# FFN down projection: weight sums formed beside the products instead of during gate/up

## The chip, the core and the metric

One core of a Trainium2 chip runs the whole program. The metric is the device time of one execution in microseconds (us), lower is better; the number compared is the median of several runs. Engines: TensorE (PE, its weight loads PEld), VectorE (DVE), ScalarE (ACT), GpSimd (POOL), and SyncE (SP), which here only issues DMAs. SPq, ACTq and POOLq are the queues on which SP, ACT and POOL issue transfers.

## The reference, cut to what matters

```
x  = x + g1 * (merged @ w_out)
xn = modulate(rmsnorm(x, norm2), sh2, sc2)
h  = gelu(causal_conv3(xn @ w_gate) + b) * (xn @ w_up)      # 1024 tokens x 2816
x  = x + g2 * (h @ w_down)                                  # w_down 2816 x 1024
out = rmsnorm(x, final_norm)
```

Everything is float32. `g2` is the last sixth of `silu(c) @ w_ada + b_ada`, a row of 1024 numbers. The layers before this point are not touched by the change.

## The kernel before, in words

Every float32 operand of a matmul is split in two: a rounded high part `h` (ACT, line 117) and the rest `l = x - h` (DVE or POOL, line 118). A product then takes three matmuls of 128x512: high by high, high by low, low by high. The large products are done on 2x2 blocks with seven block products instead of eight; for that, sums and differences of blocks are formed first.

**Gate/up** (the loop over `k` in `range(KH)`, KH = 11, lines 1281 to 1308). Each `k` computes two column groups of the gate and two of the up projection. For `k` = 0 a plain form is used, for `k` = 1 to 10 `unit_ws` (line 178 on) runs twice, 7 steps of 12 matmuls each (line 192), so 168 matmuls for each `k`. DVE forms block sums (line 149), splits (line 118), brings finished PSUM banks out (lines 164 to 173: `gp` is the gate result, `up` the up result), and does the convolution (1253) and the product with the gate (1261). POOL shares sums and splits. PE may write a bank again only when DVE or ACT has brought its content out.

Two generators run beside this, one step of each for every step of the units (`feed`, queues `side` and `rest`):

- `gate_row` (lines 1222 to 1246): the row `g2`. 16 loads of 128x512 of `w_ada` (`adaw`), each multiplied into an accumulator on DVE (`adaa`, lines 1232 and 1234), and four small matmuls (line 1242) that sum over the partitions, each followed by a DVE addition (1243) and a store.
- `down_weights` (lines 1206 to 1220), 44 times, for the FFN's down stage: two loads of `w_down` into a tile `dw` (two buffers), two DVE operations (1215, 1216), two POOL operations (1217, 1218), and a store of the four sums to the DRAM scratch `wd_scr` on POOL's queue (1219).

**Down** (lines 1312 to 1418). `w_down` is cut into blocks A11, A12, A21, A22, the hidden activations into B11 to B22. Seven products are run in the order A11·B11, A12·B21, S2·tb, S1·ta, S3·tc, S4·B22, A22·td, with S1 = A21 + A22, S2 = S1 - A11, S4 = A12 - S2, S3 = A11 - A21 read back from `wd_scr`. Each product has 11 rows `k`; a row loads a token block and a weight block (`raw`, four buffers, lines 1330 and 1331), splits both (`wh`, `wl`, eight buffers of each, so four rows), and runs 12 matmuls: three for each of four token tiles `tp` (line 1338), into four PSUM banks. The first product's banks are `x`; A12·B21 uses `y`, which shares its four banks with `z` of S1 and S4. After a product, its banks are copied (ACT) or added (DVE) into `part` tiles; `settle` (1348, 1349) multiplies by `g2` and adds to the residual rows `res`, and `finish_rows` does the final norm. The residual rows, `g2b` and `fnb` are loaded with ten DMAs of 512 KB on ACT's queue after the first product (lines 1374 to 1379).

A scheduler of the framework decides the order of the instructions on each engine from the program's order and its own time estimates; each engine then runs its list strictly in that order.

Of the kernel before, what the change touches and what calls it, by code (L numbers as in the profile page):

```python
# [20 lines left out]
P = 128  # L21
# [48 lines left out]
def trunk(ctx: ExitStack, tc: tile.TileContext, I: dict, out: bass.AP, dbg=None):  # L70
# [33 lines left out]
    wd_scr = [dram.tile([P, 4, HALF], F32, name=f"wd{k}_scr") for k in range(KH)]  # L104
# [1101 lines left out]
    def down_weights(pl, k, c):  # L1206

        w = pl.tile([P, 4, P], F32, tag="dw", bufs=2, name="dw")
        for h in range(2):
            r0 = (k + KH * h) * P  # L1210
            nc.sync.dma_start(w[:, 2 * h:2 * h + 2],
                              I["f_wdown"][r0:r0 + P].rearrange("p (h c) -> p h c", h=2)[:, :, P * c:P * c + P])
        yield
        a11, a21, a12, a22 = [w[:, j] for j in range(4)]
        dve.tensor_tensor(a21, a21, a22, op=OP.add)
        dve.tensor_tensor(a11, a21, a11, op=OP.subtract)
        pool.tensor_tensor(a22, a22, a11, op=OP.subtract)
        pool.tensor_tensor(a12, a12, a11, op=OP.subtract)
        nc.gpsimd.dma_start(wd_scr[k][:, :, P * c:P * c + P], w)
        yield  # L1220

    def gate_row(pl):

        for h in range(2):
            acc = pl.tile([P, HALF], F32, tag="adaa", bufs=1, name="adaa")
            c = 5 * D + HALF * h
            for k in range(KD):
                w = pl.tile([P, HALF], F32, tag="dw", bufs=2, name="adaw")
                nc.sync.dma_start(w, I["w_ada"][k * P:(k + 1) * P, c:c + HALF])
                yield  # L1230
                if k == 0:
                    dve.tensor_scalar(acc, w, cond[:, k:k + 1], None, op0=OP.mult)
                else:
                    dve.scalar_tensor_tensor(acc, w, cond[:, k:k + 1], acc, op0=OP.mult, op1=OP.add)
                yield
            yield
            row = pl.tile([1, 256], F32, tag="grow", bufs=1, name="grow")
            for q in range(2):
                sl = slice(256 * q, 256 * q + 256)
                nc.sync.dma_start(row, I["b_ada"][c:c + HALF][sl].rearrange("(o n) -> o n", o=1))  # L1240
                pt = gb3()
                pe.matmul(pt[0:1, :256], ones[:, 0:1], acc[:, sl], start=True, stop=True)
                dve.tensor_tensor(row, row, pt[0:1, :256], op=OP.add)
                nc.sync.dma_start(g_rows[5][:, HALF * h + 256 * q:HALF * h + 256 * q + 256], row)
                row = pl.tile([1, 256], F32, tag="grow", bufs=1, name="grow") if q == 0 else None
            yield
# [30 lines left out]
    with (tc.tile_pool(name="ffg", bufs=1) as ffg, tc.tile_pool(name="ffy", bufs=1) as ffy,  # L1277
          tc.tile_pool(name="ffu", bufs=1) as ffu, tc.tile_pool(name="ff", bufs=1) as ff):
        rest.append(gate_row(ff))
        rest.extend(down_weights(ff, k, c) for k in range(KH) for c in range(4))  # L1280
# [25 lines left out]
        while side or rest:  # L1306
# [7 lines left out]
    STEPS = (("x", "B11", "A11"), ("y", "B21", "A12"), ("x", "tb", "S2"), ("z", "ta", "S1"), ("x", "tc", "S3"),  # L1314
             ("z", "B22", "S4"), ("x", "td", "A22"))
# [6 lines left out]
    def weight_rows(n, k):  # L1322
        if n[0] == "S":
            return wd_scr[k][:, ("S2", "S1", "S4", "S3").index(n)]
# [3 lines left out]
    def down_load(tn, wn, k):  # L1328
        raw = ring.tile([P, 2, HALF], F32, tag="raw", bufs=4, name="raw")
        nc.sync.dma_start(raw[:, 0], token_rows(tn, k))  # L1330
        nc.sync.dma_start(raw[:, 1], weight_rows(wn, k))
        return raw

# [27 lines left out]

    banks = {}
    for si, (bk, tn, wn) in enumerate(STEPS[:6]):
# [8 lines left out]
        if si == 0:  # L1372
            g2b = dn.tile([P, D], F32, name="g2b")
# [4 lines left out]
            for t in range(NT):  # L1378
                nc.scalar.dma_start(res[t], x2_scr[t])
# [61 lines left out]
```

## Time and profile before

| what | value |
|---|---|
| median of 3 runs | 2039.89 us (2035.96 to 2040.68) |
| the profiled execution's own time | 2032.08 us |
| its span | 2030.2 us |
| mean granted TensorE clock | 0.97 of full |
| PE busy over the span | 1904.2 us (94%), 9503 matmuls |
| DVE busy | 1321.1 us (65%) |
| ACT busy, POOL busy | 893.1 us (44%), 945.3 us (47%) |
| DMA moved | 346.01 MB, 170 GB/s on average |

The profile is of one execution. Busy shares are means over stages with different limits. Gate/up with `unit_ws` runs from about 1360 to 1814 us after the span's start, the down stage from 1800 to the end. A wait in brackets in a timeline row is the idle time of that engine just before the instruction and what ended it. The granted clock is either 0.5 (1.2 GHz) or 1.0 (2.4 GHz) at any moment; a stretch's number is the mean.

### The profile page before, as it was taken

To read this page: it belongs to the slowest core of one execution; us is meant where nothing else is said; L and a number is where in the kernel's file an instruction comes from. 1 tells how busy PE (TensorE), PEld (TensorE's weight loads), DVE (VectorE), ACT (ScalarE), POOL (GpSimd) and SP (SyncE) were. 2 spreads that over 40 slices of the span, in tenths; PEclk is the share of its full clock that TensorE was granted. 3 is DMA by queue.
4 is the path that set the end of the run, shared out by engine and by line. 5 is a ranking of instruction groups with operands and counts; after the bars stand their busy time and mean duration, and the time that the engine had idled before them with its cause. 6 is when DMAs were issued, how large, how long until landed. Compare 5 with 4: busy or idle time off the path is not lost.

```text
span 2030.2 us, 27898 instructions
## 1 busy us (share of the span) xinstructions
PE 1904.2 (94%) x9503; PEld 1544.7 (76%) x9503; DVE 1321.1 (65%) x2215; ACT 893.1 (44%) x1638; POOL 945.3 (47%) x1265
## 2 busy tenths in 40 slices
PE   6899998999898999999999989999988899999997
PEld 5668997766676778787787769977776678887886
DVE  6776666476636673555457675679877668665567
ACT  5345556554542334544444332444333333444444
POOL 6453444354354342345556673465666666400002
PEclk9899999999999999999999999998999899999999
DMA  9233333356968554888757255314655554358654
GB/s 325 71 119 130 128 120 121 120 177 200 287 191 232 187 174 151 218 173 212 175 145 190 85 187 207 126 31 151 189 183 176 181 173 139 104 180 287 207 187 176
DMA packets 294286, 346.01 MB, mean 170 GB/s; under 512 B 19343, under 2 KB 221187, under 8 KB 294144
## 3 DMA queue, kind: packets, MB, share of 16 engines
q1 hardware_dynamic: 249616, 219.74, 36.4%
q10 hardware_dynamic: 33744, 87.18, 12.1%
q0 software_dynamic: 10784, 37.31, 6.9%
q8 instruction: 75, 1.23, 0.2%
q14 instruction: 67, 0.55, 0.1%
HBM read 244.41 MB, written 99.75 MB: 170 GB/s over the span
## 4 chain that ended last, share of the span: by engine, by line
PE 62%; DVE 12%; DMA 10%; issue 7%; POOL 5%; ACT 2%; SPq 1%; ACTq 0%; DVEq 0%; POOLq 0%
PE g L192 24%; PE gp L889 8%; PE g L1338 7%; PE go L1146 5%; PE g L267 4%; PE sl L951 3%; PE g L216 3%; DMA dw<-in_f_wdown_dram 3%; PE tp L995 2%; DVE wl L118 2%; DMA raw<-in_w_in_dram 1%; POOL wl L118 1%; DMA wd_scr<-dw 1%; PE o L1024 1%; PE o L1027 1%
## 5 line engine op out<-in xcount | busy, mean ns | idle before, releaser
L192 PE MATMUL g<-xs,wh 128*128 128x512 f32 x2520 | 821.6, 408 | 56.1 <-DVE up L169 18.0
L192 PEld LDWEIGHTS g<-xs,wh 128*128 128x128 f32 x2520 | 485.2, 194 | 189.1 <-DVE up L169 19.7
L192 PE MATMUL g<-xs,wl 128*128 128x512 f32 x1260 | 506.1, 404 | 0.0
L117 ACT ACTIVATE wh<-raw 128x512 fp32r<-128x512 f32 (+2 forms) x385 | 225.2, 609 | 345.2 <-PE g L192 77.2
L118 POOL TENSOR_TENSOR wl<-st,wh 128x512 fp32r<-128x512 f32 x153 | 240.2, 1573 | 242.7 <-ACT wh L117 234.9
L118 DVE TENSOR_TENSOR wl<-raw,wh 128x512 fp32r<-128x512 f32 (+2 forms) x284 | 226.3, 814 | 148.3 <-ACT wh L117 147.5
L192 PEld LDWEIGHTS g<-xs,wl 128*128 128x128 f32 x1260 | 244.0, 194 | 61.5 <-issue 4.2
L117 ACT ACTIVATE wh<-st 128x512 fp32r<-128x512 f32 x204 | 126.5, 629 | 266.7 <-PE g L192 167.0
L118 POOL TENSOR_TENSOR wl<-raw,wh 128x512 fp32r<-128x512 f32 (+2 forms) x101 | 137.4, 1363 | 165.2 <-ACT wh L117 154.5
L149 POOL TENSOR_TENSOR st<-raw 128x512 f32<-128x512 f32 x102 | 154.4, 1518 | 92.3 <-DVE wl L118 64.9
L889 PE MATMUL gp<-oT,wh 128*128 128x512 f32 x512 | 169.7, 412 | 0.9 <-DVE ot L173 0.9
L267 PE MATMUL g<-wh,xs 128*128 128x256 f32 x672 | 126.0, 288 | 0.0
L959 ACT ACTIVATE pm<-pm,stat 128x128 f32<-128x128 f32 (+1 forms) x192 | 89.3, 468 | 51.0 <-DVE stat L956 46.1
L1356 POOL TENSOR_TENSOR ms<-ms 128x1 f32<-128x1 f32 x8 | 4.8, 603 | 224.5 <-ACT junk L1355 224.4
L267 PEld LDWEIGHTS g<-wh,xs 128*128 128x128 f32 x672 | 104.6, 189 | 4.1 <-issue 4.1
L889 PEld LDWEIGHTS gp<-oT,wh 128*128 128x128 f32 x512 | 89.4, 191 | 21.9 <-issue 7.7
L1338 PE MATMUL g<-wl,wh 128*128 128x512 f32 x264 | 103.7, 393 | 0.0
L1338 PE MATMUL g<-wh,wl 128*128 128x512 f32 x264 | 103.6, 392 | 0.0
L889 PE MATMUL gp<-oT,wl 128*128 128x512 f32 x256 | 102.0, 398 | 0.0
L1338 PE MATMUL g<-wh 128*128 128x512 f32 x264 | 96.5, 390 | 2.1 <-ACT wh L117 2.1
L267 PE MATMUL g<-wl,xs 128*128 128x256 f32 x336 | 95.1, 283 | 0.0
L956 DVE CUSTOM_DVE_ANT_0 pm<-sl,bt 128x128 f32<-128x128 f32 (+1 forms) x192 | 64.0, 378 | 45.2 <-PE sl L951 45.0
(297 smaller groups left out, 3510.9 us busy)
## 6 DMA issues: line engine op xcount, KB each, us to landing
raw<-in_w_in_dram SPq DMA_DIRECT2D x66, 512.0 KB, 5.2
adaw<-in_w_ada_dram SPq DMA_DIRECT2D x48, 256.0 KB, 5.4
g_scr<-ot ACTq DMA_DIRECT2D x24, 512.0 KB, 3.6
raw<-in_w_ada_dram SPq DMA_DIRECT2D x24, 512.0 KB, 4.0
qk<-q_scr POOLq DMA_DIRECT2D x12, 1024.0 KB, 6.8
qk<-k_scr POOLq DMA_DIRECT2D x24, 512.0 KB, 10.2
raw<-g_scr SPq DMA_DIRECT2D x24, 512.0 KB, 3.4
raw<-in_f_wgate_dram SPq DMA_DIRECT2D x22, 512.0 KB, 5.1
```

The lines of the kernel that those rows point to most:

```text
L117: act.activation(h, src, AF.Copy)
L118: l_eng.tensor_tensor(l, src, h.bitcast(F32), op=OP.subtract)
L149: engs[int(name[1]) - 1].tensor_tensor(s_, src.get(x_) if isinstance(x_, str) else x_, src.get(y_) if isinstance(y_, str) else y_, op=op)
L192: pe.matmul(banks[bk], a[:, k, :], b, start=(fresh and j == 0), stop=(j == 11), skip_group_check=True)
L216: pe.matmul(banks[i, h], a[:, k, :], b, start=(fresh and j == 0), stop=(not fresh and j == 11), skip_group_check=True)
L267: pe.matmul(banks[t2][bk][:, 256 * i:256 * i + 256], a[:, sl], b[:, k % 2, :], start=(fresh and i == 0 and j == 0), stop=(j == 11), skip_g ...
L889: pe.matmul(pt, a_[:, k % g, :], b_, start=(j == 0), stop=(j == 3 * n - 1))
L951: pe.matmul(sb[:, of:of + n], lq, kt[:, ks], start=(of == 0 and kt is kh), stop=(kt is kl), skip_group_check=True)
L956: dve.tensor_tensor_reduce(out=pm[:, of:of + n], in0=sb[:, of:of + n], in1=bt[:, cfg, 256 - n:], scale=1.0, scalar=3e38, op0=OP.add, op1=O ...
L959: act.activation(pm[:, of:of + n], pm[:, of:of + n], AF.Exp, scale=-1.0, bias=stt[:, cfg, 0, idx:idx + 1], accum_out=stt[:, cfg, 1, idx:id ...
L1146: pe.matmul(pt[:, :256], a_[:, sl], b_[:, k % 2, :], start=(j == 0), stop=(j == 3 * KD - 1))
L1338: pe.matmul(bank, a_[:, sl], b_, start=(start and j == 0), stop=(j == 2), skip_group_check=True)
```

## The change

`down_weights` and `wd_scr` are gone: nothing of the down weights is formed in gate/up. In the down stage each row of a product with an S weight now forms its sum on DVE just ahead of its split: S1 into one of 11 tiles `held` (A21 + A22, the latter loaded into `held`), S2 and S4 in place from it, S3 in a `st` tile (three buffers) into which A21 is loaded. So that each sum follows from the one before, the products are in the order S1, S2, S4, S3. With that order `y` is followed directly by `z`, in the same banks, and `x` of S3 by `x` of A22. `gate_row` loads one tile ahead, uses a tile four steps after its load, and has three empty steps after each use. The loads of `g2b`, `fnb` and `res` are asked for one row after the end of the first product, and `settle` (with `finish_rows`) runs as a generator, one token tile for each row of the following product. The tiles `last` come from a pool that opens when `held` is closed.

```diff
-    wd_scr = [dram.tile([P, 4, HALF], F32, name=f"wd{k}_scr") for k in range(KH)]
...
-    def down_weights(pl, k, c):
...
+        def fetch(i):
+            if i < 2 * KD:
+                h, k = divmod(i, KD)
+                raws[i] = pl.tile([P, HALF], F32, tag="adaw", bufs=2, name="adaw")
+                nc.sync.dma_start(raws[i], I["w_ada"][k * P:(k + 1) * P, 5 * D + HALF * h:5 * D + HALF * h + HALF])
+        fetch(0)
+        for i in range(2 * KD):
+            h, k = divmod(i, KD)
+            fetch(i + 1)
+            for _ in range(4):
                 yield
+            w = raws.pop(i)
...
-        rest.extend(down_weights(ff, k, c) for k in range(KH) for c in range(4))
...
-    STEPS = (("x", "B11", "A11"), ("y", "B21", "A12"), ("x", "tb", "S2"), ("z", "ta", "S1"), ("x", "tc", "S3"),
-             ("z", "B22", "S4"), ("x", "td", "A22"))
+    STEPS = (("x", "B11", "A11"), ("y", "B21", "A12"), ("z", "ta", "S1"), ("x", "tb", "S2"), ("z", "B22", "S4"),
+             ("x", "tc", "S3"), ("x", "td", "A22"))
...
+    held = [sums.tile([P, HALF], F32, tag="held", bufs=KH, name="held") for _ in range(KH)]
+
+    def weight_sum(wn, k, a):
+        if wn[0] == "A":
+            return a
+        if wn == "S3":
+            s_ = ring_tmp([HALF])
+            nc.sync.dma_start(s_, block_rows("A21", k))
+            dve.tensor_tensor(s_, a, s_, op=OP.subtract)
+            return s_
+        s_ = held[k]
+        if wn == "S1":
+            nc.sync.dma_start(s_, block_rows("A22", k))
+            dve.tensor_tensor(s_, a, s_, op=OP.add)
+        elif wn == "S2":
+            dve.tensor_tensor(s_, s_, a, op=OP.subtract)
+        else:
+            dve.tensor_tensor(s_, a, s_, op=OP.subtract)
+        return s_
...
+    def residual():
+        nc.scalar.dma_start(g2b, bcast_rows(g_rows[5], P, D))
...
+    def settle_all(c, t0, sl, finish=False):
+        for tp in range(4):
+            settle(c[tp], t0 + tp, sl)
+            if finish:
+                finish_rows(t0 + tp)
+            yield
...
-            ts_, ws = ring_split(raw[:, 0], [HALF], dve), ring_split(raw[:, 1], [HALF], dve)
+            ts_ = ring_split(raw[:, 0], [HALF], dve)
+            ws = ring_split(weight_sum(wn, k, raw[:, 1]), [HALF], dve)
             for tp in range(4):
                 down_mm(banks[bk][tp], ts_, ws, tp, fresh and k == 0)
+            feed(side)
```

Three places in the built order. The first is DVE in gate/up at a place where PE waits for the `up` bank of line 169, before:

```order
L149 TENSOR_TENSOR st_14492<-st_14465,raw_14242 128x512
L1215 TENSOR_TENSOR dw_14512<-dw_14512 128x128
L1216 TENSOR_TENSOR dw_14512<-dw_14512 128x128
L1215 TENSOR_TENSOR dw_14559<-dw_14559 128x128
L1216 TENSOR_TENSOR dw_14559<-dw_14559 128x128
L169 TENSOR_TENSOR up_13883<-g3_14117,up_13883 128x512
L164 TENSOR_TENSOR gp_14232<-g3_14273,gp_14232 128x512
L171 TENSOR_TENSOR up_13883<-up_13883,g3_14191 128x512
```

and the same place of a `k` in the change (line numbers are one lower there):

```order
L148 TENSOR_TENSOR st_14346<-st_14322,raw_14127 128x512
L168 TENSOR_TENSOR up_13818<-g3_14020,up_13818 128x512
L163 TENSOR_TENSOR gp_14117<-g3_14155,gp_14117 128x512
L170 TENSOR_TENSOR up_13818<-up_13818,g3_14082 128x512
L117 TENSOR_TENSOR wl_14300<-raw_14127,wh_14299 128x512
```

The four `dw` operations between the block sum and the bank are gone. The second place is the second half of the gate row on DVE, in the change (1224 and 1226 are the lines 1232 and 1234 of before, 1239 is 1243, 1248 is 1253):

```order
L1239 TENSOR_TENSOR grow_14344<-grow_14344,g3_14387 1x256
L1224 TENSOR_SCALAR adaa_14506<-adaw_14115,cond_369 128x512
L1248 SCALAR_TENSOR_TENSOR y_14278<-gp_14118,cols1_682,y_14278 128x1024
L1248 SCALAR_TENSOR_TENSOR y_14277<-gp_14117,cols1_682,y_14277 128x1024
L1226 SCALAR_TENSOR_TENSOR adaa_14506<-adaw_14409,cond_369,adaa_14506 128x512
L148 TENSOR_TENSOR st_14655<-st_14632,raw_14440 128x512
...
L1226 SCALAR_TENSOR_TENSOR adaa_14506<-adaw_14570,cond_369,adaa_14506 128x512
L1226 SCALAR_TENSOR_TENSOR adaa_14506<-adaw_14714,cond_369,adaa_14506 128x512
L168 TENSOR_TENSOR up_14122<-g3_14328,up_14122 128x512
L170 TENSOR_TENSOR up_14122<-up_14122,g3_14395 128x512
L1226 SCALAR_TENSOR_TENSOR adaa_14506<-adaw_14874,cond_369,adaa_14506 128x512
```

All eight uses of that half stand within 19 rows of DVE (a `k` has about 30), some three `k` later than before; the eight of the first half stand in the same rows of DVE's list as before. In the program's text they are spread over nine `k`, in the built order they are not. The four small matmuls stand 451 to 1050 PE rows later than before, away from the last `adaa` operation that they read. The third place is the start of the down stage: ACT in the change (1383 to 1386 are the loads, `raw_16461` is row 7 of the first product, `raw_16484` row 8),

```order
L116 ACTIVATE wh_16445<-raw_16438 128x512
L1383 DMA g2b_16286<-g2_scr_1057 128x1024
L1384 DMA fnb_16287<-in_final_norm_dram 128x1024
L1386 DMA res_16288<-x20_scr_159 128x1024
L116 ACTIVATE wh_16464<-raw_16461 128x512
L1386 DMA res_16289<-x21_scr_160 128x1024
L116 ACTIVATE wh_16468<-raw_16461 128x512
L1257 DMA ff10_scr_177<-up_15957 128x1024
L1386 DMA res_16290<-x22_scr_161 128x1024
```

where before all ten loads stand in one piece behind the split of row 10; and SP in the change (`raw_16621` is row 2 of the second product, `raw_16644` row 3):

```order
L1322 DMA raw_16621<-ff13_scr_180 128x512
L1323 DMA raw_16621<-in_f_wdown_dram 128x512
L1341 DMA held_16275<-in_f_wdown_dram 128x512
L1341 DMA held_16276<-in_f_wdown_dram 128x512
...
L1341 DMA held_16285<-in_f_wdown_dram 128x512
L1322 DMA raw_16644<-ff14_scr_181 128x512
L1323 DMA raw_16644<-in_f_wdown_dram 128x512
```

The ten loads start four rows earlier and are mixed with splits and stores, and the eleven `held` loads stand in one piece ahead of row 3 of the second product. PE's list is the same up to single places, but for the first rows of S1·ta: there it goes bank by bank, ten matmuls for the first bank before the first one for the second.

## Rows read from the trace of the kernel before

**Rows 1.** Busy time by stretch, all engines; then PEclk, DMA share, GB/s.

```profile
core 0: us, PE busy (x) PEld busy (x) DVE busy (x) ACT busy (x) POOL busy (x), PEclk, DMA share, GB/s
...
1380.00:1440.00 60.00, 56.28 (x235) 44.19 (x235) 56.66 (x65) 22.67 (x34) 30.19 (x26) 0.97 0.59 190
1440.00:1700.00 260.00, 231.29 (x938) 182.82 (x938) 188.67 (x241) 86.38 (x134) 183.24 (x207) 0.93 0.55 172
1700.00:1800.00 100.00, 100.00 (x437) 81.69 (x436) 66.14 (x76) 41.75 (x63) 42.72 (x30) 1.00 0.37 126
1820.00:1860.00 40.00, 37.93 (x161) 30.87 (x160) 18.48 (x30) 17.46 (x31) 0.00 (x0) 0.96 0.94 343
1860.00:2000.00 140.00, 140.00 (x619) 115.97 (x618) 89.31 (x142) 69.62 (x122) 0.87 (x1) 1.00 0.62 198
```

**Rows 2.** The same view for line 192 alone (the gate/up matmuls).

```profile
1380.00:1440.00 60.00, 55.03 (x231) 43.94 (x231) 0.97 0.59 190
1440.00:1700.00 260.00, 230.21 (x934) 182.65 (x934) 0.93 0.55 172
1700.00:1800.00 100.00, 100.00 (x437) 81.65 (x435) 1.00 0.37 126
```

**Rows 3.** Waits by engine, 1440 to 1700 us: total, times, longest.

```profile
PE g L192 <- DVE up L169: 18.0, 4, 6.4
...
PE g L1242 <- DVE grow L1243: 2.5, 1, 2.5
...
DVE dw L1215 <- DMA dw<-in_f_wdown_dram: 65.3, 29, 5.8
```

**Rows 4.** Timeline of DVE and PE, 1548 to 1559 us.

```profile
1550.92 1.32 DVE L1216 TENSOR_TENSOR dw<-dw 128x128 f32<-128x128 f32 x1
1556.83 0.29 DVE L1215 TENSOR_TENSOR dw<-dw 128x128 f32<-128x128 f32 x1 [4.59 <-DMA dw<-in_f_wdown_dram]
1557.37 0.68 DVE L169 TENSOR_TENSOR up<-g,up 128x512 f32<-128x512 f32 x1
...
1558.11 1.22 PE L192 MATMUL g<-xs,wh 128*128 128x512 f32 x2 [6.38 <-DVE up L169]
```

**Rows 5.** Busy time in the stretch of half clock behind that wait.

```profile
1555.40:1562.20 6.80, 4.09 (x10) 3.23 (x11) 5.33 (x7) 0.00 (x0) 3.01 (x5) 0.50 0.37 116
```

**Rows 6.** Groups of instructions, 1395 to 1705 us, and 1300 to 1425 us (last row).

```profile
L1242 PE MATMUL g<-adaa,ones 128*1 128x256 f32 x8 | 2.6, 432 | 4.7 <-DVE grow L1243 2.5 <-DVE adaa L1234 2.2
...
L118 DVE TENSOR_TENSOR wl<-raw,wh 128x512 fp32r<-128x512 f32 x27 | 30.9, 1144 | 0.0
...
L149 DVE TENSOR_TENSOR st<-st,raw 128x512 f32<-128x512 f32 x4 | 6.0, 1508 | 0.0
```

**Rows 7.** Groups of instructions, 1700 us to the end.

```profile
L118 DVE TENSOR_TENSOR wl<-raw,wh 128x512 fp32r<-128x512 f32 x141 | 92.3, 689 | 76.4 <-ACT wh L117 76.3
...
L117 ACT ACTIVATE wh<-raw 128x512 fp32r<-128x512 f32 x145 | 85.4, 627 | 113.4 <-PE g L1338 71.7 <-PE g L192 20.2 <-DMA res<-x_scr 10.6
...
L1349 DVE TENSOR_TENSOR res<-res,c 128x512 f32<-128x512 f32 x12 | 8.3, 690 | 0.0
```

**Rows 8.** Timeline of ACT at the residual loads, then a DVE row behind them.

```profile
1816.52 1.32 ACT L117 ACTIVATE wh<-raw 128x512 fp32r<-128x512 f32 x2 [2.08 <-PE g L1338]
...
1829.06 7.41 ACTq L1379 DMA_DIRECT2D res<-x_scr  x8
1836.57 3.24 ACT L117 ACTIVATE wh<-raw 128x512 fp32r<-128x512 f32 x6 [10.59 <-DMA res<-x_scr]
...
1848.75 4.81 DVE L118 TENSOR_TENSOR wl<-raw,wh 128x512 fp32r<-128x512 f32 x7 [1.29 <-ACT wh L117]
```

**Rows 9.** Line 1338 by stretch: the gap, the half clock, an undisturbed product.

```profile
1835.30:1837.80 2.50, 0.43 (x3) 0.03 (x1) 1.00 1.03 418
1838.70:1842.10 3.40, 3.40 (x10) 2.65 (x9) 0.50 1.02 407
1869.20:1899.20 30.00, 30.00 (x134) 24.82 (x134) 1.00 0.64 194
```

**Rows 10.** DMA issues, 1820 to 1860 us, then 1860 to 2000 us (last row): median us to landing.

```profile
res<-x_scr ACTq DMA_DIRECT2D x8, 512.0 KB, 9.1
...
raw<-in_f_wdown_dram SPq DMA_DIRECT2D x11, 256.0 KB, 4.8
```

More of the change, by code (lines that the diff above doesn't have):

```diff
@@ L1222, in gate_row @@
-    def gate_row(pl):
[L1224 to L1229, printed above, removed]
-                yield
[L1231 to L1234, printed above, removed]
+    def gate_row(pl):
+        raws = {}
+        def fetch(i):
[8 more added lines that the diff above has]
+            for _ in range(4):
+                yield
+            w = raws.pop(i)
+            if k == 0:
+                acc = pl.tile([P, HALF], F32, tag="adaa", bufs=1, name="adaa")
+                dve.tensor_scalar(acc, w, cond[:, k:k + 1], None, op0=OP.mult)
+            else:
+                dve.scalar_tensor_tensor(acc, w, cond[:, k:k + 1], acc, op0=OP.mult, op1=OP.add)
+            for _ in range(3):
@@ L1235, in gate_row @@
                 yield
-            yield
-            row = pl.tile([1, 256], F32, tag="grow", bufs=1, name="grow")
+            if k < KD - 1:
+                continue
             for q in range(2):
-                sl = slice(256 * q, 256 * q + 256)
-                nc.sync.dma_start(row, I["b_ada"][c:c + HALF][sl].rearrange("(o n) -> o n", o=1))
+                c = HALF * h + 256 * q
+                row = pl.tile([1, 256], F32, tag="grow", bufs=1, name="grow")
+                nc.sync.dma_start(row, I["b_ada"][5 * D + c:5 * D + c + 256].rearrange("(o n) -> o n", o=1))
+                yield
+                yield
@@ L1241, in gate_row @@
                 pt = gb3()
-                pe.matmul(pt[0:1, :256], ones[:, 0:1], acc[:, sl], start=True, stop=True)
+                pe.matmul(pt[0:1, :256], ones[:, 0:1], acc[:, 256 * q:256 * q + 256], start=True, stop=True)
                 dve.tensor_tensor(row, row, pt[0:1, :256], op=OP.add)
-                nc.sync.dma_start(g_rows[5][:, HALF * h + 256 * q:HALF * h + 256 * q + 256], row)
-                row = pl.tile([1, 256], F32, tag="grow", bufs=1, name="grow") if q == 0 else None
-            yield
+                nc.sync.dma_start(g_rows[5][:, c:c + 256], row)
@@ L1248, in conv @@
+                yield
     def conv(k, gp, ys):
@@ L1360, in finish_rows @@
             nc.sync.dma_start(out[0, t * P:(t + 1) * P, dsl], res[t][:, dsl])
+    g2b = dn.tile([P, D], F32, name="g2b")
+    fnb = dn.tile([P, D], F32, name="fnb")
+    res = [dn.tile([P, D], F32, tag="res", bufs=NT, name="res") for _ in range(NT)]
+    cs = {}
+    def residual():
+        nc.scalar.dma_start(g2b, bcast_rows(g_rows[5], P, D))
+        nc.scalar.dma_start(fnb, bcast_rows(I["final_norm"], P, D))
+        for t in range(NT):
+            nc.scalar.dma_start(res[t], x2_scr[t])
+        yield
+    def settle_all(c, t0, sl, finish=False):
[3 more added lines that the diff above has]
+                finish_rows(t0 + tp)
+            yield
     banks = {}
@@ L1406, in trunk @@
         for i in range(2):
-            h, l = [dn.tile([P, HALF], F32R, tag="last", bufs=4 * KH, name="last") for _ in range(2)]
+            h, l = [lp.tile([P, HALF], F32R, tag="last", bufs=4 * KH, name="last") for _ in range(2)]
             split_to(h, l, raw[:, i], dve)
```

64 lines of the change are left out of this document (20 added, 44 removed).

## The prediction

> **What bounds the kernel now.** I first read the busy time by stretch. PE is the engine to follow, since it works nearly without a gap where nothing disturbs it: in 1700 to 1800 us it is busy for the whole of 100 us at clock 1.00 and runs 437 gate/up matmuls of line 192 [rows 1, 2], so one takes 100 / 437 = 0.229 us. Held against that rate the other stretches show what they lose. In 1440 to 1700 there are 934 such matmuls, worth 934 x 0.229 = 213.7 us, so **46.3 us are lost**; in 1380 to 1440 there are 231, worth 52.9, so 7.1 are lost [rows 2]. POOL and DMA are busier there, DVE at 189 of 260 us is not full, and the clock is 0.93 and 0.97 [rows 1].
>
> Next the waits say who causes it. In 1440 to 1700, PE waits four times, 18.0 us in all, for DVE's line 169, which empties the up bank. DVE itself stands 65.3 us in 29 waits at line 1215, for the `dw` loads [rows 3]. The timeline joins the two: DVE waits 4.59 us for a `dw` load at 1556.83, line 169 stands right behind it on the same engine, and PE has been idle 6.38 us when it gets its bank [rows 4]. DVE takes its list in order, so a load asked for too late stops a bank that had nothing to do with it. The loss does not end there: in the 6.8 us that follow PE runs at clock 0.50, 1.2 GHz: busy 4.09 us, it does 10 matmuls where the undisturbed rate gives 30 [rows 5]. So the 46.3 us are the waits, the half clock behind them, and PE held at DVE's pace while it catches up.
>
> Last, the down stage. An undisturbed product there (132 matmuls) is worth 132 x 30 / 134 = 29.6 us, a row of 12 about 2.7 [rows 9], with DVE busy 89 of 140 us and POOL with a single instruction [rows 1]. Its one visible loss is near the second product: a gap of 2.5 us with three matmuls, then 3.4 us at clock 0.50 [rows 9], beside ten residual loads of 512 KB that take 9.1 us to land [rows 10] and that ACT stood 10.59 us for [rows 8]. PE is idle 2.07 us of 1820 to 1860 [rows 1], and 3.4 us at half clock lose 1.7: 3.8 us.
>
> **The change, part by part.**
>
> *The `dw` steps go.* 44 times two loads, two DVE and two POOL operations and a store. The engines' own time costs nothing: in 1700 to 1800 DVE does its block sums and evacuations without `dw` and PE loses nothing [rows 1]. What goes is the wait. Of the 46.3 us I take away what the gate row causes there and not `dw`: its small matmuls, 8 records of 432 ns [rows 6], half of them in this stretch, 1.7; its wait of 2.5 [rows 3]; and half of a half-clock stretch like the one of 3.4 us in rows 9, 1.7. That leaves 46.3 - 5.9 = 40.4. In the built order the up bank now follows the block sum directly, and behind neither stands an operation that waits for a load just asked for. **-40.4.**
>
> *The gate row.* It loses 5.9 in the one stretch and 7.1 in the other, 13.0 in all. The 3.5 us of the matmuls stay. Of the other 9.5 the earlier loads and the distance of the four matmuls from the last `adaa` should take all, but in the built order the second half stands bunched on DVE, each multiplication within a few rows of the next load, so a `dw`-like wait or two is left there. Bounds 0 and -9.5, between which no row decides; the middle, **-4.7**.
>
> *The start of the down stage.* The ten loads now start near 1818 (ACT splits of that row stand at 1816.52 [rows 8]). Before PE can start row 3 of the second product, near 1845, the queues must bring ten residual loads (5.2 MB), the store of the last activations (0.5) and of four token sums (1.05), eleven `held` loads of 256 KB (2.9), which stand on SP's queue ahead of that row's own loads, and five raw rows (2.6): 12.3 MB in 27 us. At the mean of 343 GB/s of 1820 to 1860 [rows 1] that takes 36 us, at the 407 to 418 of the worst moments [rows 9] about 30: PE is 3 to 9 us late. I take 5, the nearer to the high rate since the queue stands full, plus 1.7 for half clock behind it, against the 3.8 lost there now: **+2.9**. Bounds: -3.8 if nothing is late, and 9 + 3.4 - 3.8 = +8.6 at the mean rate with two stretches of half clock.
>
> The Trainium skill, "DMA: Bandwidth & Descriptors", section Specifications, gives a limit of about 358 GB/s for HBM for each core, which speaks against this part of the change. By it the 12.3 MB would take an estimated 34.4 us, PE would be 7.4 late, the term +5.3 and the time 2002. The trace does not agree for short stretches: 418 and 407 GB/s stand in rows 9; over 40 us its 343 is below that limit.
>
> *The sums in the down stage.* 44 DVE operations on 128x512, for which the nearest rows are the split (689 ns) and the residual addition (690 ns) of this stage [rows 7]; 7 splits in one go took 4.81 us [rows 8]. A row of an S product has three of them, 2.07 us, under the row's 2.7, so it is hidden behind PE; DVE is otherwise idle there 76.4 us for ACT [rows 7]. With all the rest: DVE's 89.3 in 140 us is 76.5 for four products of 120 us, and 44 x 0.69 = 30.4 more makes 107 of 120. That holds on average, with little over where the bank additions and a settled token tile stand in one row. Two places are tight. `y` and `z` share banks without a product between them, so S1's first rows wait for DVE's additions bank by bank. And S3 loads into one of three `st` buffers: 4.8 us to landing [rows 10] + 0.69 + 0.63 of ACT [rows 7] + 0.69 = 6.8 for three rows, 2.3 for each, below 2.7. **+2**, bounds 0 and +10 (a gap of 2.5 with its half clock at two or three boundaries). The loads of `wd_scr` are replaced one for one by loads of `w_down`, which costs nothing there; the products are still seven, and the end is A22 as before.
>
> **Sum:** -40.4 - 4.7 + 2.9 + 2.0 = -40.2. The profiled execution took 2032.1 us (its span of 2030.2 and 1.9 around it), so 1991.9; it was 7.8 below the median of 2039.9, against which I forecast **1999.7**. About 0.3%, 6 us, is what a measurement of this kernel can tell from no change.
>
> **The rivals.**
>
> *Next in line.* DVE's wait goes, but another operation ahead of line 169 takes its place: beside POOL a block sum takes 1508 ns and a split 1144, against 689 without it [rows 6, 7]. If half of the 40.4 comes back, the sum is -20.0, the time 2020. For it: those rows, and POOL's 183 of 260 us in the stretch of the losses [rows 1], of which only the two operations of each `dw` step go. Against it: with POOL at work 43 of 100 us, 1700 to 1800 loses nothing [rows 1]. 8 in 100.
>
> *Loads starve the start of down.* If the burst runs at the 198 GB/s of 1860 to 2000 [rows 1], 12.3 MB take 62 us and PE is 35 late; in place of the +2.9 stands 35 + 1.7 - 3.8 = 32.9, in sum -10.2, 2030. Against it: the rate of 343 beside the same queues; those 198 were what was wanted, not what could be had. 4 in 100.
>
> *Slower: DVE bounds the S products.* This decides when its mean operation there reaches 1.21 us: then a row takes 3.63, 0.92 over PE's 2.71, and 44 x 0.92 = 40 eats the gain. At the 1508 ns of rows 6 it would be 44 x (4.52 - 2.71) = 80 in place of the +2, in sum +37, **2077**. For it: DVE's share of 107 in 120 us. Against it: those long operations stand beside POOL, and POOL runs one instruction in 140 us of the down stage [rows 1]. 4 in 100.
>
> *It does not do what it says.* In the stretch of the losses DVE may be late for its own bank work, `dw` only the last to be seen; then waits move to line 169 itself and 2040 stays. Against it: the bank of rows 4 was due while DVE stood idle, and DVE is only 189 of 260 us busy [rows 1]. 4 in 100.
>
> **How the numbers follow.** The forecast has 80 in 100, the rivals 20. Its best end is -40.4 - 9.5 - 3.8 + 0 = -53.7 (1986), its worst -40.4 - 0 + 8.6 + 10 = -21.8 (2018); with the 4 us or less by which the runs shown lie below their median, and up to the first rival, the range is 1982 to 2021. It takes in the forecast and about half of that rival. Faster: forecast, next in line and starving, 92; the same 4; slower 4.
>
> **What would show it.** Gate/up: near 437 matmuls of line 192 in 100 us in all of 1380 to 1780, clock near 1.00, no DVE wait for a load but one or two at the gate row's second half. If PE's waits for line 169 stay at 10 us or more, next in line is right. Start of down: near the second product a PE gap of 3 to 9 us with a half clock behind it, SP's eleven loads ahead of it, GB/s over 343; over 15 us means starving. S products: about 30 us each, sums of 690 ns, PE waiting for DVE under 1 us apart from S1's first row; a sum of over 1.2 us means the slower rival. It is wrong if the stretch of 260 us gets back less than 30 us, or if the four S products take over 10 us more than four undisturbed ones.

## The result, and the profile after

| | before | changed |
|---|---|---|
| median of 4 runs | 2037.93 us (2035.96 to 2040.68) | 2006.28 us (2004.11 to 2008.72) |
| the profiled execution's own time, its span | 2032.08, 2030.2 | 2004.11, 2002.4 |
| up to the first matmul of gate/up k = 1 | 1360.1 | 1367.8 |
| from there to the last gate/up matmul | 453.4 | 408.3 |
| from there to the last matmul of down | 205.3 | 216.7 |
| from there to the end | 11.3 | 9.6 |

The ratio is 0.9847, 95% interval 0.983 to 0.9865, so the change takes 31.7 us off, clear of noise. The forecast was 1999.7, 40.2 below the median of 2039.9; the measured 2006.28 is 6.6 above it, inside the range of 1982 to 2021. The stages that the change touches became 45.1 - 11.4 + 1.7 = 35.4 us shorter. The 7.6 us by which gate/up starts later are not its doing: up to the gate row, in gate/up, PE's list of instructions is the same, and in the profiles of this case, all of one program up to there, that first matmul stands anywhere from 1360.1 to 1373.9 us. The kernel before was profiled in an execution 5.9 us below its median and at the low end of this; a sum made against it inherits that.

In gate/up the loss of the long stretch is gone. By stretch, the columns being those of rows 1:

```profile
1440.00:1700.00 260.00, 260.00 (x1127) 210.51 (x1126) 173.58 (x197) 106.28 (x159) 123.92 (x94) 1.00 0.34 110
```

PE is busy for the whole stretch at clock 1.00, where rows 1 had 231.29 us and 0.93. Note POOL: 124 us and 94 instructions against 183 and 207. The ends of line 191 (192 before) in both kernels, before and changed, give the 453.4 and 408.3 (shortest, median, longest ns; first and last start; the very last matmul is one with `wl`, about 0.2 us after the last one with `wh`):

```profile
L192 PE MATMUL g<-xs,wh x1120: 387/393/796, 1360.1 to 1813.3; 128*128 128x512 f32 x187
```

```profile
L191 PE MATMUL g<-xs,wh x1120: 387/392/501, 1367.8 to 1775.8; 128*128 128x512 f32 x187
```

The down stage pays. The same stretch view of the changed kernel:

```profile
1786.00:1795.00 9.00, 9.00 (x41) 7.46 (x40) 2.59 (x4) 1.90 (x4) 0.00 (x0) 1.00 1.03 417
1795.00:1801.00 6.00, 1.39 (x5) 0.88 (x4) 1.29 (x2) 1.58 (x3) 0.00 (x0) 0.74 1.04 408
...
1813.00:1818.00 5.00, 1.43 (x6) 0.86 (x5) 1.73 (x3) 2.30 (x4) 0.00 (x0) 1.00 0.94 327
1870.40:1900.10 29.70, 29.70 (x133) 24.59 (x131) 21.85 (x35) 14.45 (x27) 0.00 (x0) 1.00 0.60 196
```

Two gaps, near 1795 and 1813, at a DMA share of 0.94 to 1.04, where the kernel before had one [rows 9]. In the last row an S2 product runs at full pace with its sums. With each gap goes a stretch at clock 0.50, of 6.8 and 3.4 us, in which PE (line 1353) works 4.6 and 3.4:

```profile
1797.86:1804.69 6.83, 4.61 (x11) 3.64 (x12) 0.50 1.02 375
1818.34:1821.75 3.41, 3.41 (x10) 2.66 (x9) 0.50 0.81 260
```

The timeline of the queues and ACT says why PE stands:

```profile
1798.88 1.15 ACT L116 ACTIVATE wh<-raw 128x512 fp32r<-128x512 f32 x2 [7.66 <-DMA raw<-ff_scr]
...
1801.69 6.00 SPq L1341 DMA_DIRECT2D held<-in_f_wdown_dram  x11
1808.85 0.33 SPq L1322 DMA_DIRECT2D raw<-ff_scr  x1
```

First ACT waits 7.66 us for a raw row whose transfer stands beside the residual loads (the run with these loads spread tests that below); then the eleven `held` loads keep SP's queue 6 us, and the next raw row is asked for at 1808.85. A third gap is new. PE's waits in the down stage of the changed kernel (total, times, longest):

```profile
PE g L1353 <- ACT wh L116: 8.2, 2, 4.6
PE g L1353 <- DVE c L1419: 2.6, 1, 2.6
```

The second line is before the last product: S3 and A22 both run on `x`, and PE may go on only when DVE has added S3's bank. By products the first two take 8.5 us more than before and the last 2.9, together the 11.4.

### The profile page after: what moved, and what is told of

Its sections match the earlier page's. It is cut to its first block, busy times and chain, and to the rows that moved or that the text cites. A ratio compares the mean times of both kernels' runs of the same rounds, so it can differ in the third digit from the quotient of the medians.

```text
span 2002.4 us, 27413 instructions
## 1 busy us (share of the span) xinstructions
PE 1887.5 (94%) x9503; PEld 1535.3 (77%) x9503; DVE 1300.0 (65%) x2171; ACT 896.7 (45%) x1638; POOL 857.1 (43%) x1133
## 5 line engine op out<-in xcount | busy, mean ns | idle before, releaser
L191 PE MATMUL g<-xs,wh 128*128 128x512 f32 x2520 | 807.8, 402 | 41.9 <-DVE ot L168 11.1
L191 PEld LDWEIGHTS g<-xs,wh 128*128 128x128 f32 x2520 | 477.1, 191 | 169.6 <-DVE ot L168 12.8
L191 PE MATMUL g<-xs,wl 128*128 128x512 f32 x1260 | 499.7, 399 | 0.1
L116 ACT ACTIVATE wh<-raw 128x512 fp32r<-128x512 f32 (+2 forms) x341 | 202.1, 607 | 353.7 <-PE g L191 88.9
L191 PEld LDWEIGHTS g<-xs,wl 128*128 128x128 f32 x1260 | 239.8, 190 | 59.5 <-issue 3.4
L117 DVE TENSOR_TENSOR wl<-raw,wh 128x512 fp32r<-128x512 f32 (+2 forms) x240 | 186.5, 783 | 120.0 <-ACT wh L116 119.6
L116 ACT ACTIVATE wh<-st 128x512 fp32r<-128x512 f32 x215 | 133.4, 628 | 264.4 <-PE g L191 168.2
## 6 DMA issues: line engine op xcount, KB each, us to landing
qk<-k_scr POOLq DMA_DIRECT2D x24, 512.0 KB, 10.1
```

The source lines that it names most:

```text
L116: act.activation(h, src, AF.Copy)
L117: l_eng.tensor_tensor(l, src, h.bitcast(F32), op=OP.subtract)
L191: pe.matmul(banks[bk], a[:, k, :], b, start=(fresh and j == 0), stop=(j == 11), skip_group_check=True)
```

## Experiments: what in the dw steps cost gate/up 45 us

All lengths are from the first matmul of gate/up k = 1 to the last one, read as above. The first six kernels tell the parts of the `dw` steps apart; a seventh, the changed kernel with the old gate row, is the zero that they are held against.

**No loads.**

```diff
-            nc.sync.dma_start(w[:, 2 * h:2 * h + 2],
...
-        dve.tensor_tensor(a21, a21, a22, op=OP.add)
-        dve.tensor_tensor(a11, a21, a11, op=OP.subtract)
...
+        dve.tensor_tensor(a21, ident, ones, op=OP.add)
+        dve.tensor_tensor(a11, a21, ident, op=OP.subtract)
...
```

> The kernel before, with the two loads of each dw step left out: the sums are formed from two constant tiles, so the S weights and the output are not the reference's. The two DVE and two POOL operations, the store and their places in the program stay; only the load that DVE waited for is gone (with its traffic). Measured in the profile from the first matmul of unit_ws (k = 1) to the last gate/up matmul: 453.4 us in the kernel before, 408.3 in the changed one. Theory (the loss is DVE standing in order behind a load just asked for): 40 us less, 410 to 418 us, no wait of PE for line 169 over 1 us, time near 1998. Rival next in line (DVE's and POOL's work for dw is itself what makes the bank late): half or less comes back, 430 to 445 us, time 2015 to 2030.

Measured: 443.3 us and a median of 2028.14, ratio 0.9941 (0.9922 to 0.996). The ends of its line 192:

```profile
L192 PE MATMUL g<-xs,wh x1120: 387/393/797, 1368.4 to 1811.5; 128*128 128x512 f32 x187
```

The theory of the prediction falls: 10 us, not 40, and these 10 are for the wait and the traffic of the loads together. The waits in 1440 to 1700 us of this run show what stands there now:

```profile
PE g L192 <- DVE gp L169: 14.4, 5, 5.7
...
DVE dw L1211 <- DMA wd_scr<-dw: 13.8, 11, 2.0
```

PE waits for the same line of DVE. Over the whole of gate/up, first the kernel before and then this run, DVE does the same number of operations, 410:

```profile
1360.14:1813.55 453.41, 417.43 (x1724) 332.65 (x1723) 340.97 (x410) 168.32 (x259) 271.85 (x271) 0.95 0.49 157
1368.37:1811.70 443.33, 413.15 (x1725) 329.63 (x1723) 350.12 (x410) 168.90 (x259) 270.68 (x271) 0.97 0.42 134
```

It is busy 9.2 us longer with them, and its idle time falls by 19.2 us only, from 112.4 to 93.2, although 65.3 us of waits for loads are gone. The other 46 us came back as other waits: 13.8 for the store of the tile that the next sum is to be written into (the row above), 20.0 in place of 10.3 for POOL's splits, and smaller ones behind ACT and PE.

**Loads asked for earlier.** Nothing is left out; with two tiles, a load can go out only when an earlier step's store has freed its tile.

```diff
...
+            nc.gpsimd.dma_start(wd_scr[k][:, :, P * c:P * c + P], w)
+            yield
+            fetch(i + 2)
+            yield
```

> The kernel before, nothing left out, with the dw loads asked for two steps of the generator earlier, right behind the store that frees their tile. Theory: the wait shrinks by what the load is earlier. A tile's round is load 5.5 us, DVE 0.6, POOL about 1, store about 5, some 12 us for two tiles, 6 for each step, and a step comes every 8.7 us on average but in bunches, so part of the wait is left: 415 to 430 us from the first unit_ws matmul to the last gate/up matmul (453.4 before), time 1998 to 2015. Rival next in line: 435 us or more. Rival that the stretch is slow whatever dw does: 453.

Measured: 455.4 us, 2039.63, ratio 1.0 (0.998 to 1.002). DVE still waits 57.7 us for these loads in 1440 to 1700, in 27 waits. SP's own waits in that stretch, first in the kernel before and then in this one, say why nothing moved:

```profile
SPq L1211 <- DMA wd_scr<-dw: 137.1, 42, 7.8
SPq L1216 <- DMA wd_scr<-dw: 135.7, 39, 8.0
```

Already in the kernel before SP stands at the next `dw` load until a store has freed the tile, so the load could not go out earlier. The wait that the prediction read as a load asked for too late is one for a free tile, with two tiles in turn; its loads and stores landed 3.0 us after their issue in the median (2.4 to 6.1), not the 5.5 and 5 of the expectation. This run does not tell the rivals apart.

**No POOL part, DVE alone, POOL alone, POOL's operations alone.** In the four, the down stage reads plain blocks of `w_down`.

```diff
-        pool.tensor_tensor(a22, a22, a11, op=OP.subtract)
-        pool.tensor_tensor(a12, a12, a11, op=OP.subtract)
-        nc.gpsimd.dma_start(wd_scr[k][:, :, P * c:P * c + P], w)
```

> The kernel before, with POOL's part of each dw step left out: its two subtractions and the store. Loads and the two DVE operations stay; the down stage reads plain blocks of w_down in place of the stored sums, so the output is not the reference's. Taking the loads away gave only 10.1 of the 45.1 us of gate/up (443.3 against 453.4 and 408.3), and in that run DVE operations of 0.69 us stand at 2 to 4.4 us beside back-to-back POOL operations. New theory (DVE is held up by POOL's work for dw, and each hold-up reaches the bank): most comes back although DVE still waits for loads, 410 to 425 us. Theory of the prediction (the load wait is the loss): the waits stay and so does the time, 440 to 453 us.  Third (DVE simply has too much in its list, waits included): between, 425 to 440.

The second is this on top of the edit without loads; the third keeps POOL's subtractions, on constant tiles, and the store of half the tile, and drops loads and DVE's lines:

> The kernel before with loads and POOL's part of the dw steps both left out; only the two DVE operations of 128x128 stay, on constant tiles. The output is not the reference's. If the loss needs a partner of DVE (a load to wait for, or POOL's work beside it), nothing is lost: 408 to 412 us for gate/up. If DVE's own list is too long, 88 operations of 0.29 us are 26 us of work, of which part shows: 415 us or more.

> The kernel before with loads and DVE's part of the dw steps left out: POOL's two subtractions (on constant tiles) and the store of half the tile stay. DVE runs nothing for dw and waits for nothing of it; the output is not the reference's. New theory (POOL's added operations hold up DVE's others): a part of the loss is there with no dw operation on DVE at all, 418 to 440 us for gate/up, with DVE operations of over 2 us. If it needs DVE's own dw operations, 408 to 412.

The fourth is the third without its store:

```diff
-        nc.gpsimd.dma_start(wd_scr[k][:, 2:4, P * c:P * c + P], w[:, 2:4])
```

> The kernel before with only the two POOL subtractions of each dw step left (on constant tiles), without store, loads and DVE operations; the output is not the reference's. With the store it was 429.3 us for gate/up, 21.1 over the kernel without dw. In that run POOL spends 0.72 + 0.84 us on the subtractions and 0.73 on issuing the store, and DVE operations between SBUF tiles stand still over all three. Theory (DVE is held up by any unbroken chain of POOL work): the loss falls with POOL's time by about a third or more, 415 to 423 us. Rival (only arithmetic on POOL holds up DVE): 427 to 430. Rival (the store's traffic or its place on POOL's queue is the loss): 408 to 412.

| kernel | of dw it keeps | gate/up, us | over the kernel without dw | median, ratio with interval |
|---|---|---|---|---|
| before | loads, DVE, POOL, store | 453.4 | 45.2 | |
| no_dw_loads | DVE, POOL, store | 443.3 | 35.1 | 2028.14, 0.9941 (0.9922 to 0.996) |
| no_pool_part | loads, DVE | 427.3 | 19.1 | 2012.82, 0.9886 (0.9865 to 0.9907) |
| pool_only | POOL, half the store | 429.3 | 21.1 | 2011.41, 0.9874 (0.9848 to 0.9901) |
| pool_ops | POOL | 428.6 | 20.4 | 2014.05, 0.9884 (0.9847 to 0.9921) |
| dve_only | DVE | 416.5 | 8.3 | 2003.97, 0.9839 (0.9814 to 0.9865) |
| old_gate_row | nothing | 408.2 | 0 | 2006.79, 0.9839 (0.9819 to 0.986) |

The rows of no_pool_part, pool_only, pool_ops, dve_only and old_gate_row that the table rests on, in this order:

```profile
L191 PE MATMUL g<-xs,wh x1120: 387/392/797, 1368.8 to 1795.9; 128*128 128x512 f32 x187
```

```profile
L192 PE MATMUL g<-xs,wh x1120: 387/392/797, 1362.8 to 1791.8; 128*128 128x512 f32 x187
```

```profile
L192 PE MATMUL g<-xs,wh x1120: 389/392/797, 1371.2 to 1799.6; 128*128 128x512 f32 x187
```

```profile
L191 PE MATMUL g<-xs,wh x1120: 387/392/632, 1363.9 to 1780.3; 128*128 128x512 f32 x187
```

```profile
L191 PE MATMUL g<-xs,wh x1120: 387/392/628, 1368.5 to 1776.4; 128*128 128x512 f32 x187
```

The parts nearly add up. The loads cost 45.2 - 35.1 = 10.1 with all the rest there, and 19.1 - 8.3 = 10.8 with DVE alone, where DVE's waits for them come to 30.5 us only, since no store holds the tile. DVE's 88 operations cost 8.3, POOL's 88 subtractions 20.4, and half the store, whose issue takes POOL 0.73 us each time, 0.7 more; DVE's and POOL's together make 35.1, which is 5.7 over their sum. Each length is of one profile: the changed kernel's gate/up, left as it is in four more runs, took 408.3 to 409.7, so 0.7 cannot be told from nothing. Two things limit the reading. The scheduler packs shortened steps more densely, so the loss falls in fewer `k`; the totals are compared, not the places. And while `dw` steps are there, the gate row's tiles share their two buffers; in old_gate_row they have two of their own.

How POOL's work reaches the bank is seen in pool_only, in which DVE runs nothing for `dw`. Two pieces of its timeline:

```profile
1437.51 1.45 POOL L1213 DMA_DIRECT2D wd_scr<-dw  x2
...
1438.04 2.78 DVE L1266 TENSOR_TENSOR y<-up,y 128x512 f32<-128x512 f32 x1
1438.98 1.27 POOL L118 TENSOR_TENSOR wl<-st,wh 128x512 fp32r<-128x512 f32 x1
...
1442.37 0.69 DVE L169 TENSOR_TENSOR gp<-g,gp 128x512 f32<-128x512 f32 x1 [1.55 <-ACT gp L168]
...
1443.12 1.22 PE L192 MATMUL g<-xs,wh 128*128 128x512 f32 x2 [4.20 <-DVE gp L169]
```

```profile
1550.49 4.66 DVE L118 TENSOR_TENSOR wl<-raw,wh 128x512 fp32r<-128x512 f32 x1
1550.81 1.30 POOL L149 TENSOR_TENSOR st<-raw 128x512 f32<-128x512 f32 x1
1552.05 0.46 POOL L1211 TENSOR_TENSOR dw<-ident,ones 128x128 f32<-128x128 f32 x1
1552.47 0.46 POOL L1212 TENSOR_TENSOR dw<-ones,ident 128x128 f32<-128x128 f32 x1
1552.89 1.28 POOL L118 TENSOR_TENSOR wl<-raw,wh 128x512 fp32r<-128x512 f32 x1
1554.14 0.45 POOL L1211 TENSOR_TENSOR dw<-ident,ones 128x128 f32<-128x128 f32 x1
```

An operation of this shape, which takes DVE 0.69 us in the down stage [rows 7], takes 2.78 and 4.66 us here, as long as POOL works without a break, and line 169 comes late behind it. The `dw` operations close the breaks in POOL's list. DVE also waits for POOL's own splits, which become late: 39.1 us in 13 waits in 1440 to 1700 of this run, against 30.8 in 13 of the changed kernel, where none of them costs PE anything. That second way is the longest wait of pool_ops:

```profile
1509.98 3.82 DVE L149 TENSOR_TENSOR st<-raw,st 128x512 f32<-128x512 f32 x1 [9.11 <-POOL wl L118]
...
1517.87 1.22 PE L192 MATMUL g<-xs,wh 128*128 128x512 f32 x2 [6.65 <-ACT up L166]
```

POOL's split stands behind its `dw` subtractions, DVE waits 9.11 us for it, and after DVE's and ACT's next operations PE has been idle for 6.65. Over gate/up of pool_only, pool_ops and old_gate_row DVE is busy 320, 296 and 286 us with 322 operations:

```profile
1362.79:1792.07 429.28, 409.79 (x1725) 327.97 (x1723) 320.18 (x322) 169.39 (x259) 278.79 (x271) 0.98 0.39 125
1371.21:1799.80 428.59, 407.83 (x1725) 328.55 (x1724) 295.55 (x322) 170.93 (x259) 240.93 (x227) 0.97 0.34 112
1368.51:1776.67 408.16, 399.76 (x1724) 323.43 (x1723) 285.57 (x322) 171.67 (x259) 189.13 (x139) 1.00 0.37 119
```

So DVE is slowed by 34.6 us in the first and by 10.0 in the second, and both lose 20 to 21: the loss does not follow the slowing of DVE alone. How it divides between the two ways is not shown.

**The old gate row in the changed kernel.** `gate_row` as in the kernel before, with its tiles under the tag `adaw`.

```diff
-            for _ in range(4):
...
+                w = pl.tile([P, HALF], F32, tag="adaw", bufs=2, name="adaw")
+                nc.sync.dma_start(w, I["w_ada"][k * P:(k + 1) * P, c:c + HALF])
                 yield
...
```

> The changed kernel with gate_row as it was before (load, one step, use; the four small matmuls right behind). Theory of the prediction: the gate row's new form gave 4.7 (bounds 0 and 9.5), so gate/up takes 408.3 + 5 to 10 = 413 to 418 us and PE waits for adaa and grow 2 to 5 us as before; time 2011 to 2016. Rival (the gate row's waits were dw's doing, since both share their queue and two tiles): 408 to 410, time as the changed kernel.

Measured: 408.2 us. The rival holds: the new form of the gate row is worth nothing here. PE waits 2.1 us for `adaa` once, and k = 1 takes 49.9 us where it takes 46.4 in the changed kernel; but there three later `k` take 40.1, 39.4 and 39.4 us where the old form has 38.7. The new form spreads the loss and does not remove it.

## Experiments: the down stage

Lengths are from the last gate/up matmul to the last matmul of all: 216.7 us in the changed kernel. In old_gate_row, with the same text for this stage, it was 219.0, so differences of 2 us between single profiles say nothing here.

**No sums.**

```diff
-        if wn[0] == "A":
-            return a
+        return a
```

> The changed kernel with the sums of the down stage left out: each S product takes the first block alone as its weight, so the output is not the reference's; the 11 held loads, the 11 st loads and 44 DVE operations are gone. Theory from the two traces (the second gap at the start of the down stage is the 11 held loads standing on SP's queue ahead of row 3; the sums themselves are hidden): the gap of 4.0 us in the second product and its 3.4 us at half clock go (35.2 to about 30 us), the first product's gap of 5.0 stays, S products stay at 29.7 us; the gap of 3.0 before A22 stays or shrinks; time 5 to 8 below the changed kernel. Rival (the first gap too is the held loads' traffic, or the sums bound the S products): both gaps go, 12 us or more below.

Measured: 209.0 us, median 1999.36, ratio 0.9798 (0.9773 to 0.9823). PE's waits in the down stage:

```profile
PE g L1351 <- ACT wh L116: 4.5, 1, 4.5
PE g L1351 <- DVE c L1417: 1.1, 1, 1.1
```

The second product falls to 29.9, the first keeps a gap of 4.5 us, the S products stay at 29.9 with or without sums. Within the products the sums' arithmetic therefore costs nothing; their first loads cost 5.5 us (35.4 to 29.9 in the second product). The wait before A22 is 1.1 us here and 2.6 in the changed kernel; in the profile of old_gate_row it was 4.0, so that the sums cause this difference is not shown.

**The residual loads spread.** Each load is tied by a one-column POOL copy to the raw tile of a row of the second or third product; they go on SP's queue.

```diff
-        for t in range(NT):
-            nc.scalar.dma_start(res[t], x2_scr[t])
-        yield
...
+            pool.tensor_copy(d[:, :1], src[:, :1])
+            nc.sync.dma_start(d, s_)
...
+            residual(k + KH * (si - 1), raw[:, 0])
```

> The changed kernel with the ten residual loads moved to SP's queue, one for every other row of the second and third product; a one-column POOL copy from that row's raw tile into the target keeps each load from starting earlier. Nothing is left out. Theory (the first gap of 5.0 us and its 6.8 us at half clock come from the ten loads in one go taking the transfer rate from the raw loads of rows 8 to 10): the first product falls from 42.2 to about 35 us, the second keeps its held gap (35.4), the down stage goes from 216.7 to 207 to 211 us, the time 2006 to about 1999. Rival (the stage's bytes have to come anyway, so a later load only moves the gap): first product 35 but the second 40 or more, no gain.

Measured: 209.5 us, median 1998.42, ratio 0.9808 (0.9779 to 0.9837). The first product is back at 35.1 and the second takes 29.9: both gaps are gone. The `held` one was expected to stay; it went too, since SP's list now has the `held` loads between the rows. PE's waits in the down stage:

```profile
PE g L1353 <- DVE c L1417: 3.6, 1, 3.6
PE g L1353 <- DVE wl L117: 2.0, 2, 1.5
```

Some is given back: 2.0 and 0.8 us in the third and fourth product, and 2.5 in the last, whose wait is 3.6 in place of 2.6, with half clock behind it.

**The last product in banks of its own.**

```diff
-            down_mm(banks["x"][tp], ts_, ws, tp, False)
+            down_mm(banks["z"][tp], ts_, ws, tp, ts_ is last[0][0])
...
+            dve.tensor_tensor(d, banks["x"][tp], g2b[:, hi], op=OP.mult)
+            dve.tensor_tensor(res[tp][:, hi], res[tp][:, hi], d, op=OP.add)
```

> The changed kernel with the residual loads spread (as in the run before) and, second, the last product A22*td in the banks of z, started afresh, instead of on top of S3's x; what stands in x is multiplied by g2 and added to the residual rows by DVE (8 operations) beside the last product. Nothing is left out. Theory (PE waits before A22 for DVE's additions out of x, which stand behind splits for A22 in DVE's list: 3.0 us in the changed kernel, 4.0 and half clock in the spread one): the last product falls from 35.3 to about 30 us, down stage from 209.5 to 204 to 206, time about 1993. Rival (DVE has too much to do there: the splits of A22 themselves are late once the bank is free): last product 32 us or more.

Measured: 205.1 us and a last product of 29.9, as the theory says, but the tail, from the last matmul to the end, grew from 9.1 to 15.6 us, more than the 4.4 that PE gained, and the median is 1999.93, ratio 0.9815 (0.9781 to 0.9849); about 1993 was expected. DVE's eight extra operations, 8 x 0.69 = 5.5 us, stand among the final norms and are of that size; that they alone make the tail longer was not tried.

**S1 through the ring as well.**

```diff
-            nc.sync.dma_start(s_, block_rows("A22", k))
-            dve.tensor_tensor(s_, a, s_, op=OP.add)
+            t_ = ring_tmp([HALF])
+            nc.sync.dma_start(t_, block_rows("A22", k))
+            dve.tensor_tensor(s_, a, t_, op=OP.add)
```

> As spread_own_banks, and besides the second block of S1 is loaded into one of the three st tiles, and the sum written into held from there, so that its load cannot be asked for eleven rows ahead. Theory: the 1.9 us lost in the third product of the spread run (DVE waits 5.4 us for a held load) goes or stays as small, since three tiles allow three rows ahead: down stage within 2 us of spread_own_banks. Rival (the long lead was what kept S1 fed): S1's product 2 us or more longer.

Measured: 209.2 us, S1's product 37.6 (33.7 in the run above), median 2003.49, ratio 0.9825 (0.9782 to 0.9868). The rival holds, and the timeline shows the very pattern of rows 4 in the down stage: a sum waits for its load, the addition out of `y`'s bank stands behind it, PE waits.

```profile
1836.51 0.69 DVE L1343 TENSOR_TENSOR held<-raw,st 128x512 f32<-128x512 f32 x1 [2.63 <-DMA raw<-in_f_wdown_dram]
...
1837.72 0.68 DVE L1425 TENSOR_TENSOR c<-c,g 128x512 f32<-128x512 f32 x1
...
1838.55 0.76 PE L1354 MATMUL g<-wh 128*128 128x512 f32 x1 [5.02 <-DVE c L1425]
```

Of all versions the spread one has the lowest median of those that compute everything, but its interval meets that of the changed kernel; its gain is shown by the profile (7.2 us in the down stage), not by the times alone.

## Why the prediction was right, and where it was not

**Gate/up: the total right, the cause not.** -40.4 and -4.7 were forecast, 45.1 us came. The step that failed is "The engines' own time costs nothing ... What goes is the wait": the loads, wait and traffic, are worth 10 to 11 us, DVE's two operations 8, POOL's two subtractions 20, DVE and POOL together 6 more. The total held because the change takes every part of `dw` away, so the loss of the stretch was the right number whichever part caused it; it says nothing for the mechanism. The wait of 65.3 us [rows 3] was real, but without it gate/up is 10.1 us shorter, DVE works 9.2 us longer, and 46 us of other waits take its place. Nor was it "a load asked for too late": SP asked as soon as the tile was free. The rows that showed it were read: a split of 1144 ns against 689 [rows 6, 7]. They were set aside because 1700 to 1800 us loses nothing, a stretch with POOL at 43 of 100 us; the stretch with the loss had 183 of 260.

**The rival "next in line"** had read the rows that matter, operations that take longer beside POOL, but did not come. It held that the rest of POOL's work would keep up half the loss, with "only the two operations of each `dw` step" gone; these two are 20 of the 45 us, and without them and DVE's two the stretch loses nothing. In no_dw_loads, where they stay, 35 of 45 us stayed.

**The gate row:** -4.7 forecast, +0.1 measured (bounds 0 and -9.5). The step that failed is the one that split the loss of the stretch between it and `dw`: 5.9 and 7.1 us were charged to it, of which the rows show waits of 2.5 and 2.2 at its lines [rows 3, 6]; the 7.1 were the whole loss of 1380 to 1440, without a row that made it the gate row's. Taking its waits away moves the loss and leaves it. That `dw` gave 45.2 in place of 40.4 makes up for it: the two misses cancel, which is luck.

**The start of the down stage:** +2.9 forecast, +8.5 measured, at the upper bound of +8.6. The transfers do come late by the size in the working (PE idle 4.6 and 3.6 us), but in two gaps, each with its own half clock (PE works 4.6 + 3.4 us in it, of which about half is lost, 4.0), where one gap near 1845 with one half-clock stretch was forecast; 8.2 + 4.0 less the 3.8 lost before makes 8.4 of the 8.5. The first gap is at the end of the first product, for which the working had no term: it counted bytes up to one row and not what each row before it needs. The limit of about 358 GB/s for HBM in the Trainium skill, "DMA: Bandwidth & Descriptors", section Specifications, does not show here: 417 GB/s stand over 9 us ahead of the first gap. residual_spread shows that the bytes fit; when and in what order they were asked for cost the time.

**The sums:** +2 forecast (0 to +10). Within the products the arithmetic costs nothing, as said: 687 to 692 ns each and products of 29.9 us. The tight boundary was put at `y` and `z`, where PE lost nothing; it is at S3 and A22, both on `x`, 2.9 us, which the prediction passed over with "the end is A22 as before".

**The tail** became 1.7 us shorter, with `settle` done earlier; no term stood for it, and its cause was not tried. These three terms make up 5.6 + 0.9 - 1.7 = 4.8 of the 8.5 us by which less than 40.2 came; the rest lies in the executions that are compared, ahead of these stages. **Slower** and **it does not do what it says** did not come: with POOL idle in the S products DVE keeps its 690 ns.

## What to carry to other kernels

A wait in the trace is a place, not yet a price: take away the wait alone and see whether other waits and slower work fill the time, before the whole loss is charged to it. Where two engines slow each other, the price of a side task is not its own busy time: it slows the other engine's operations and makes the main work behind it on its own engine late. So compare an operation's duration with and without company, and look for what waits behind it, before calling the work hidden. Before asking for a load earlier, see whether the queue is already standing for its tile. And before moving loads, write down for each row when its own load is due; bytes that fit over a stage still cost a gap if one queue has them in the wrong order.

## What the runs showed of the hardware

DVE operations with both sources in SBUF can be held up by POOL; those that read a PSUM bank were not. The groups on DVE, in 1414 to 1650 us of pool_only:

```profile
L118 DVE TENSOR_TENSOR wl<-raw,wh 128x512 fp32r<-128x512 f32 x23 | 32.3, 1404 | 0.0
L1255 DVE TENSOR_TENSOR up<-up,y 128x1024 f32<-128x1024 f32 x12 | 25.1, 2095 | 0.1
...
L1265 DVE TENSOR_TENSOR y<-up 128x512 f32<-128x512 f32 x6 | 7.1, 1180 | 0.0
...
L173 DVE TENSOR_TENSOR up<-g,up 128x512 f32<-128x512 f32 x6 | 4.1, 682 | 0.8 <-PE g L192 0.8
```

and in 1440 to 1690 us of the changed kernel, with POOL's `dw` work gone:

```profile
L117 DVE TENSOR_TENSOR wl<-raw,wh 128x512 fp32r<-128x512 f32 x26 | 19.3, 743 | 0.0
L1256 DVE TENSOR_TENSOR up<-up,y 128x1024 f32<-128x1024 f32 x12 | 14.6, 1218 | 0.0
L1266 DVE TENSOR_TENSOR y<-up 128x512 f32<-128x512 f32 x6 | 10.7, 1775 | 0.0
...
L172 DVE TENSOR_TENSOR up<-g,up 128x512 f32<-128x512 f32 x6 | 4.1, 690 | 11.1 <-PE g L191 11.1
```

The split goes from 1404 to 743 ns and the product with the gate from 2095 to 1218; the lines that read `g` (PSUM) stay at 680 to 692 in either. Not every group gets shorter: the difference of two `up` halves (lines 1265 and 1266) goes from 1180 to 1775 ns, with PE at full pace. A long operation is thus not by itself a price. The Trainium skill, "SBUF — State Buffer", section "SBUF: two separate sides", says that DVE, when both inputs are in SBUF, and GpSimd share a pair of ports as an exclusive lock that one holds for a whole instruction. The rows agree on who is held up. They show more than one instruction's length, though: the 4.66 us above span five POOL operations that follow each other, 1550.81 to 1554.59, and DVE did not get in between. Elsewhere in this run the two alternate, and DVE loses little:

```profile
1435.43 0.95 DVE L1261 TENSOR_TENSOR y<-up,y 128x512 f32<-128x512 f32 x1
...
1435.79 0.91 POOL L1211 TENSOR_TENSOR dw<-ident,ones 128x128 f32<-128x128 f32 x1
```

What decides between the two is not shown.
